# An SSM stage reordered: input tables ahead of output tables, an earlier forget gate, and stores issued by GpSimd

## The chip, the cores and the metric

One core of one Trainium2 chip runs the whole kernel. The metric is the device time of one execution in microseconds; a comparison goes by the median of several runs. Engines are named as the profile names them: PE is TensorE (matrix products), DVE is VectorE, ACT is ScalarE, POOL is GpSimd, SP is SyncE, which only issues transfers. ACT and POOL can issue transfers too; the profile writes an issue from ScalarE as ACTq, from SyncE as SPq.

## The reference

One block of a streaming encoder on 1024 rows and 16 meta rows (L = 1040) of width 1024: a root-mean-square norm, one large input projection, two mixers beside each other, gates, an output projection, and a gated feed-forward part with a short convolution. What matters here is the mixer:

```python
def _mixer(xn, w_in, b_forget, w_attn_out, lam_re, lam_im, b_re, ..., w_glu, w_o):
    proj = xn @ w_in
    q, k, v, f_logit, u, gates = jnp.split(proj, SPLITS, axis=-1)
    y_a = _forgetting_attention(q, k, v, f_logit, b_forget) @ w_attn_out
    z = jax.nn.gelu(_s5(u, lam_re, lam_im, b_re, b_im, c_re, c_im, d_skip, log_dt))
    zg = z @ w_glu
    y_s = zg[..., :D_MODEL] * jax.nn.sigmoid(zg[..., D_MODEL:])
    g = jax.nn.sigmoid(gates)
    merged = g[..., :D_MODEL] * y_a + g[..., D_MODEL:] * y_s
    return merged @ w_o
```

`_forgetting_attention` adds F[t] - F[s] to the logits, where F is the running sum of log sigmoid(f_logit + b_forget). `_s5` is a diagonal complex state space model (SSM): 32 groups of 16 channels with 64 complex states each, x_t = lam_bar x_(t-1) + b_bar u_t and y_t = Re(C x_t) + D u_t.

## The kernel before

Every matrix product of full precision is made of three products of rounded parts (xhi·whi, xlo·whi, xhi·wlo: `dense_steps`, lines 159 to 161, one "gate matmul" each below). The rounded weight whi is made by ScalarE from a loaded copy (raw, lines 140 and 146); its remainder wlo by a second load that GpSimd issues and that is added on top (`lo_by_dma`, lines 135 and 136). `split_lo` (line 129) is the same remainder made by VectorE or GpSimd. Since many places call it, its rows in the profile are told apart by the names of their tiles.

The stretch of interest lies between about 75 and 262 us.

- The **SSM input** u has been written to memory (u_d, line 394: steps 0 and 2 of it from SyncE, 1 and 3 from GpSimd).
- The **SSM** runs over the 32 groups in four steps qt = 0 to 3 of eight groups. In each, `tables` builds on VectorE two kinds of tables: the output tables Gm and Tm (16 matmuls of Gm with bA on line 1692 give Kt, copied by ScalarE on 1694; Tm is zeroed by GpSimd and filled by eight transfers of Kt from SyncE on 1702), and the input table (Vm, transposed by TensorE on 1713 and copied to Wi by ScalarE on 1714), and the decay dt8 (a copy on line 1716). `chain` loads U from u_d (1724), multiplies it with Wi (16 products, 1730, copied to wr and wi), runs the recurrence over the chunks on VectorE (two scans, and the complex rotations rot), and forms Y = Gm·St + Tm·U (1770 and 1772), its GELU, and the store y_d.
- The **gate chunks** are the dense work: eight chunks of 128 output channels, each three blocks of 342 columns with 24 matmuls: 576 in all. A sigmoid (443) and a store to g_d (444) follow every block. The SSM's products are mixed into this stream.
- Behind them stand **q and k** of the first pair of heads (`project_qk`, 144 matmuls), the **forget gate** (`forget`, lines 511 to 531: 48 products with wf, then Exp, Ln and a scan) and the **GLU** with w_glu, in the form of seven products of sums and differences of blocks of z and of the weights (`glu`, `seven`, lines 219 to 221; the weights' parts are the tiles ops, line 578).
- `load_z` (543 to 567) reads y_d back as zt in four pieces m, each by eight transfers, rounds them to zhi (548) with remainder zlo, forms the differences zf (558 to 561) and splits them in z1h, z1l, z2h and so on.

The order of instructions on each engine isn't the order of the text: a scheduler interleaves them at build time by priority and by its own estimate of what is ready, and `after` adds an order by hand. Every engine then executes its own list strictly in that order. A transfer's issue may wait for an older transfer, as there are a limited number of lanes by which their completion is told.

Of the kernel before, what the change touches and what calls it, by code (L numbers as in the profile page):

```python
# [19 lines left out]
P = 128  # L20
# [5 lines left out]
H = 8  # L26
# [24 lines left out]
def block_kernel(ctx, tc, x, meta, g1, x0t, g1t, w_q, w_k, w_v, w_f, w_u, w_g, b_f, w_ao, lam_d, bw_d, cw_d,  # L51
# [76 lines left out]
    def split_lo(eng, out_, src, hi):  # L128
        return eng.tensor_tensor(out_, src, hi.bitcast(F), ALU.subtract)  # L129
# [36 lines left out]
    def run(gen):  # L166
        for _ in gen:
            pass
# [234 lines left out]
        after(ld, queue[-1])  # L403
    next(ssm_steps)
    after(ssm_log[n_log], ready)
    ssm_tables, ssm_chain = next(ssm_steps)


    chains = {}

    def begin(q):
        ssm_tables(q)
        chains[q] = ssm_chain(q)
        next(chains[q])

    begin(0)
    begin(1)
    for q in range(4):
        run(chains[q])
        if q < 2:  # L420
            begin(q + 2)
    st_u.close()
    st_n.close()


    st_g = ExitStack()
    gp_ = pool(st_g, "gates", side="right")

# [2 lines left out]
    def gate_chunk(i, pl, tanh):  # L431
        whi, wlo = gate0[1:] if i == KD else wchunk(w_g[i], KD, GP, act=not tanh)
        if tanh:
            gs = pl.tile([P, LQ], F, tag="gs", name="gs", bufs=1)
        for t, n in QBLK:
            ps = mm_ps()
            yield from dense_steps(ps[:, :n], whi, wlo, xhi[:, :, T0 + t:T0 + t + n],
                                   xlo[:, :, T0 + t:T0 + t + n], KD)
            if tanh:
                S.activation(gs[:, t:t + n], ps[:, :n], AF.Tanh, scale=0.5)  # L440
            else:
                gs = pl.tile([P, LQ // 3], F, tag="gs", name="gs", bufs=2)
                S.activation(gs, ps[:, :n], AF.Sigmoid)
                S.dma_start(g_d[P * i:P * i + P, t:t + n], gs)
        if tanh:
            GP.tensor_scalar(gs, gs, 0.5, 0.5, ALU.mult, ALU.add)
            if pl is not gp_ and i == KD - 1:
                okeep["g"] = gs
            else:
                SY.dma_start(g_d[P * i:P * i + P], gs)  # L450
# [2 lines left out]
        run(gate_chunk(i, gp_, False))  # L453
    st_g.close()
    st_s.close()
    st_f = ExitStack()
    fp = pool(st_f, "fgate", side="right")
    fraw = fp.tile([P, KD, H], F, name="fraw")
    wf = fp.tile([P, KD, 64], R, name="wf")
    bf = fp.tile([H, 1], F, name="bf")  # L460

    def forget_w():
        SY.dma_start(fraw, w_f)
        SY.dma_start(bf, b_f.unsqueeze(1))
        GP.memset(wf.bitcast(F), 0.0)
        GP.tensor_scalar(wf[:, :, :H], fraw, 1.0, 0.0, ALU.mult, ALU.add)
        split_lo(GP, wf[:, :, 32:32 + H], fraw, wf[:, :, :H])

    st_k = ExitStack()
    qps = [pool(st_k, "qkA", side="left")]

# [34 lines left out]
    def zblock(r, h_):  # L508
        return [t_[:, 2 * r:2 * r + 2, TH * h_:TH * h_ + TH] for t_ in (zhi, zlo)]

    def forget():

        fl_ = gz.tile([P, L], F, tag="gl", name="fl_", bufs=2)[:H]
        fx = gz.tile([P, L], F, tag="gl", name="fx", bufs=2)[:H]
        for t, n in BLK:
            ps = mm_ps()
            for i in range(KD):
                PE.matmul(ps[:64, :n], wf[:, i, :], xhi[:, i, t:t + n], start=(i == 0), stop=False)
                PE.matmul(ps[:64, :n], wf[:, i, :], xlo[:, i, t:t + n], start=False, stop=(i == KD - 1))
            S.copy(fx[:, t:t + n], ps[32:32 + H, :n])  # L520
            V.scalar_tensor_tensor(out=fl_[:, t:t + n], in0=ps[:H, :n], scalar=bf, in1=fx[:, t:t + n],
                                   op0=ALU.add, op1=ALU.add)
        V.scalar_tensor_tensor(out=fx, in0=fl_, scalar=-1.0, in1=fl_, op0=ALU.mult, op1=ALU.max)
        S.activation(fx, fx, AF.Exp, scale=-1.0)
        S.activation(fx, fx, AF.Ln, bias=one[:H])
        V.scalar_tensor_tensor(out=fx, in0=fl_, scalar=0.0, in1=fx, op0=ALU.min, op1=ALU.subtract)
        V.tensor_tensor_scan(fl_, one[:H].broadcast_to([H, L]), fx, 0.0, ALU.mult, ALU.add)
        GP.tensor_scalar(fx, fl_, -8.0, 0.0, ALU.mult, ALU.add)
        SY.dma_start(f_d, fx)
        if "f_d" in dbg:  # L530
            SY.dma_start(dbg["f_d"], fx)

    def fold(t_):
        return t_.rearrange("p (n j) -> p j n", j=CH)

    def load_z():
        zts = []
        for m in range(4):
            tag = "gl" if m % 2 else "ms"
            zt = gz.tile([P, CH, NCH], F, tag=tag, name="zt", bufs=2)  # L540
            ym = y_d[m].rearrange("(j c) g n -> g c j n", c=GC)
            for g in range(GQ):
                SY.dma_start(zt[GC * g:GC * g + GC], ym[g])
            zts.append(zt)
        for m in range(4):
            w_ = NC2 if m < 2 else NCH
            zh, zl = (fold(t_[:, m, :CH * w_]) for t_ in (zhi, zlo))
            S.copy(zh, zts[m][:, :, :w_])
            split_lo(V, zl, zts[m][:, :, :w_], zh)

        def part(r, h_, k):
            return zts[2 * r + k][:, :, NC2 * h_:NC2 * h_ + NC2]

        T4 = zblock(0, 1)
        for k in range(2):
            fa, fb = (gz.tile([P, L], F, tag="cg", name="zf", bufs=2) for _ in range(2))
            f1, f2, f3, f4 = (fold(f_[:, TH * q:TH * q + TH]) for f_ in (fa, fb) for q in range(2))
            V.tensor_tensor(f1, part(0, 1, k), part(0, 0, k), ALU.subtract)
# [44 lines left out]

    n_used = [0]
    T4 = load_z()
    forget_w()
    qk = qk_tiles(0)
    run(project_qk(0, qk))
    forget()
    st_f.close()  # L610
    slots = []
    for q in range(4):
        t_ = wp.tile([P, 2, 2, 2, P], R, tag="wlo" if q % 2 else "whi", name="ops")
# [831 lines left out]
def ssm(tc, after, sp, s_ps, ident, u_d, y_d, lam_d, bw_d, cw_d, d_sk, l_dt):  # L1445
# [18 lines left out]
    def big(tag, shape, name=None):  # L1464
        return sp.tile(shape, F, tag=tag, name=name or tag, bufs=bufs[tag])
# [19 lines left out]
    def rest():  # L1485
# [183 lines left out]
        HQ = GQ // 2  # L1669
        state = {}  # L1670

        def tables(qt):
            g0 = qt * GQ
            Gm = big("Gm", [P, GQ, CH + 1, GC])
            tm = big("tq", [P, GQ, CH + 1, GC], "tm")

            def bcx(t_, n):
                return t_[:, g0:g0 + GQ].unsqueeze(2).broadcast_to([P, GQ, n, GC])
# [1 line left out]
            def bcp(t_, n):  # L1680
                return t_[:, :n, g0:g0 + GQ].rearrange("p t g -> p g t").unsqueeze(3).broadcast_to([P, GQ, n, GC])

            TT(Gm, bcx(cA, CH + 1), bcp(pr, CH + 1), ALU.mult)
            TT(tm, bcx(cB, CH + 1), bcp(pi, CH + 1), ALU.mult)
            TT(Gm, Gm, tm, ALU.subtract)
# [14 lines left out]
            GP.memset(Tm, 0.0)  # L1700
            for j in range(CH):
                SY.dma_start(Tm[16 * j:16 * (j + 1), :, 16 * j:], Kt[:, :, :P - 16 * j])

            Vm = big("tq", [P, GQ, CH, GC], "Vm")
            tv = big("tq", [P, GQ, CH, GC], "tv")
            TT(Vm, bcx(bA, CH), bcp(qr, CH), ALU.mult)
# [3 lines left out]
            for q in range(GQ // 4):  # L1710
# [1 line left out]
                for i in range(4):  # L1712
                    PE.transpose(wt[:, P * i:P * i + P], Vm[:, 4 * q + i].rearrange("p t c -> p (t c)"), ident)
                S.copy(Wi[:, 4 * q:4 * q + 4].rearrange("p g m -> p (g m)"), wt)
            dt8 = big("dt8", [P, HQ, NCH])
            V.tensor_copy(dt8, dec[:, qt * HQ:qt * HQ + HQ].unsqueeze(2).broadcast_to([P, HQ, NCH]))
            GP.memset(dt8[:, :, 0:1], 0.0)
            state[qt] = (Gm, Tm, Wi, dt8)

        def chain(qt):  # L1720
            g0 = qt * GQ
            Gm, Tm, Wi, dt8 = state.pop(qt)
            U = big("U", [P, GQ, NCH])
            SY.dma_start(U, u_d[qt])
            wr, wi = (big(n, [P, HQ, NCH]) for n in ("wr", "wi"))
            for e in range(2):
                for q in range(0, HQ, 2):
# [5 lines left out]
                    S.copy(wr[64 * e:64 * e + 64, q:q + 2], w3[:64])  # L1733
                    S.copy(wi[64 * e:64 * e + 64, q:q + 2], w3[64:])
            yield
            rc, rs = (t_[:, qt % 2 * HQ:qt % 2 * HQ + HQ] for t_ in rot[qt // 2])
            ta, tb = (big(n, [P, HQ, NCH]) for n in ("ta", "tb"))
            TT(ta, wr, rc, ALU.mult)
# [14 lines left out]
            for part, (op, fa, fb) in enumerate(((ALU.subtract, wr, ta), (ALU.add, ta, wr))):  # L1753
# [3 lines left out]
                for e in range(2):  # L1757
                    r_ = slice(64 * e, 64 * e + 64)
                    TT(S4[64 * part:64 * part + 64, :, e, 1:], x_[r_, :, :NCH - 1], y_[r_, :, :NCH - 1], op)
            if qt == 0:  # L1760
                n_ = len(log)
                rot.append(rotation(1))
                after(log[n_], log[n_ - 1])
            Y = big("sy", [P, GQ, NCH], "Y")
            for q in range(0, GQ, 3):
                nq = min(3, GQ - q)
# [5 lines left out]
                    PE.matmul(yo, Tm[:, q + i, :], U[:, q + i, :], start=False, stop=True)  # L1772
                S.copy(Y[:, q:q + nq].rearrange("p a n -> p (a n)"), yps[:, :NCH * nq])
            S.activation(Y, Y, AF.Gelu_apprx_tanh)
            S.dma_start(y_d[qt], Y)

        yield tables, chain

    return log, loads, rest()

# [56 lines left out]
```

## Time and profile before

| | us |
|---|---|
| runs before | 1481.59, 1489.31, 1491.31 (median 1489.31) |
| profiled execution, first to last instruction (span) | 1485.7 |
| TensorE busy | 1440.4 (97%), 9712 matmuls |
| VectorE busy | 1071.4 (72%) |
| ScalarE busy | 712.2 (48%) |
| GpSimd busy | 742.1 (50%) |

The profiled execution's own device time isn't listed beside its span; the median of the runs is 3.6 us above that span. "Busy" counts the time in which an instruction of the engine runs; matmuls overlap, so the time of one (0.32 us) is longer than its step (about 0.16 us). PEclk is the clock that TensorE was granted, as a share of full speed. In the lists of waits a row says who waited, for which instruction, for how long in all, how often and how long at most.

### The profile page before, as it was taken

Reading aid. Unit: us, or ns where it says so; the run is one execution under the profiler, and the core shown is the slowest. Engines: PE = TensorE matmul, PEld = TensorE weight load, DVE = VectorE, ACT = ScalarE, POOL = GpSimd, SP = SyncE. Lnnn points to the kernel's source line nnn. Section 1 sums busy time; section 2 is a strip of 40 time slices with the busy share of each in tenths; the row PEclk is TensorE's granted clock in tenths of the full one; section 3 lists DMA queues with packets and bytes.
Section 4 is the critical chain, followed back from the end, with each engine's and each line's share of the span. In section 5 each row is a group of like instructions: output and inputs, shape, how many; then the busy total and the mean of one; then the engine's idle time right before and its main releaser. Section 6 shows DMA issues by size and latency. Waiting matters only on the chain. (4 is left out here: it accounts for less than half of the span.)

```text
span 1485.7 us, 26584 instructions
## 1 busy us (share of the span) xinstructions
PE 1440.4 (97%) x9712; PEld 1358.8 (91%) x9712; DVE 1071.4 (72%) x2173; ACT 712.2 (48%) x1384; POOL 742.1 (50%) x850
## 2 busy tenths in 40 slices
PE   7999997999999999999999999999999999998997
PEld 7989996998899999999888999999999999777886
DVE  6879648881566676647468987888877776788785
ACT  6434675541555665543546534444444445543433
POOL 1311125752456465524863144455544426789766
PEclk9999999999999999999999999999999999999999
DMA  6366571551127342047885135676653215765513
GB/s 246 86 157 157 128 163 50 177 160 43 48 79 178 93 111 90 26 148 256 257 158 185 57 109 141 178 199 188 174 143 100 84 57 180 286 203 148 168 40 114
DMA packets 91032, 206.72 MB, mean 139 GB/s; under 512 B 14651, under 2 KB 25531, under 8 KB 90517
## 3 DMA queue, kind: packets, MB, share of 16 engines
q1 hardware_dynamic: 69380, 159.73, 32.9%
q0 software_dynamic: 15296, 34.63, 13.2%
q10 hardware_dynamic: 6224, 10.65, 1.9%
q8 instruction: 77, 1.26, 0.3%
q14 instruction: 55, 0.44, 0.1%
HBM read 165.90 MB, written 69.35 MB: 158 GB/s over the span
## 5 line engine op out<-in xcount | busy, mean ns | idle before, releaser
L159 PE MATMUL mm<-xhi,whi 128*128 128x342 f32 (+2 forms) x488 | 159.4, 327 | 1.0 <-DVE q L129 1.0
L161 PE MATMUL mm<-xhi,wlo 128*128 128x342 f32 (+2 forms) x488 | 158.3, 325 | 0.0
L160 PE MATMUL mm<-xlo,whi 128*128 128x342 f32 (+2 forms) x488 | 157.7, 324 | 0.0
L1079 POOL TENSOR_TENSOR ov<-ov,og 128x1024 f32<-128x1024 f32 x21 | 51.1, 2434 | 125.6 <-ACT og L1078 121.7
L129 DVE TENSOR_TENSOR sw<-sf,sw 128x512 fp32r<-128x512 f32 x72 | 66.6, 925 | 50.0 <-ACT sw L1070 49.8
L1070 ACT CAST sw<-sf 128x512 fp32r<-128x512 f32 x72 | 44.9, 624 | 106.2 <-POOL sf L1196 74.5
L159 PEld LDWEIGHTS mm<-xhi,whi 128*128 128x128 f32 x488 | 91.9, 188 | 2.1 <-PE sp L714 0.8
L161 PEld LDWEIGHTS mm<-xhi,wlo 128*128 128x128 f32 x488 | 91.8, 188 | 0.3
L160 PEld LDWEIGHTS mm<-xlo,whi 128*128 128x128 f32 x488 | 91.9, 188 | 0.2
L763 ACT CAST th<-tp 128x256 fp32r<-128x256 f32 (+3 forms) x120 | 56.2, 472 | 62.5 <-PE tp L756 30.1
L129 DVE TENSOR_TENSOR tl<-tp,th 128x256 fp32r<-128x256 f32 (+3 forms) x120 | 65.2, 547 | 25.1 <-ACT th L763 23.7
L1196 POOL TENSOR_TENSOR sf<-raw,sf 128x512 f32<-128x512 f32 x36 | 59.1, 1641 | 44.8 <-DVE sw L129 44.7
L1196 POOL TENSOR_TENSOR sf<-raw 128x512 f32<-128x512 f32 x36 | 48.0, 1332 | 66.9 <-DMA raw<-in_w_up_dram 35.9
L221 PE MATMUL mm<-xhi,sw 128*128 128x258 f32 (+1 forms) x288 | 81.0, 281 | 0.0
L219 PE MATMUL mm<-xhi,sw 128*128 128x258 f32 (+1 forms) x288 | 80.8, 281 | 0.0
L220 PE MATMUL mm<-xlo,sw 128*128 128x258 f32 (+1 forms) x288 | 80.7, 280 | 0.0
L728 POOL TENSOR_SCALAR pt<-pt,nm 128x144 f32<-128x144 f32 (+4 forms) x72 | 51.8, 731 | 48.5 <-DVE nm L727 47.5
L1248 DVE SCALAR_TENSOR_TENSOR ov<-hv,cwt,ov 128x1024 f32<-128x1024 f32 x36 | 72.5, 2014 | 0.1
L1070 ACT CAST sw<-raw 128x512 fp32r<-128x512 f32 x70 | 43.0, 621 | 53.3 <-PE sp L221 25.5
L726 ACT ACTIVATE pt<-pt,nm 128x144 f32<-128x144 f32 (+4 forms) x72 | 52.9, 735 | 26.1 <-DVE nm L725 25.7
L719 DVE CUSTOM_DVE_ANT_0 pt<-sp,fb 128x328 f32<-128x328 f32 (+8 forms) x112 | 46.4, 430 | 20.0 <-PE sp L714 11.1
L756 PE MATMUL tp<-ident,pt 128*128 128x128 f32 (+1 forms) x360 | 58.3, 270 | 0.1
(708 smaller groups left out, 5702.1 us busy)
## 6 DMA issues: line engine op xcount, KB each, us to landing
raw<-in_w_up_dram SPq DMA_DIRECT2D x44, 512.0 KB, 3.6
t_d<-in_w_dn_dram POOLq DMA_DIRECT2D x44, 256.0 KB, 7.0
ar<-a_d SPq DMA_DIRECT2D x44, 256.0 KB, 5.1
wr<-t_d SPq DMA_DIRECT2D x44, 256.0 KB, 2.8
a_d<-ov SPq DMA_DIRECT2D x21, 512.0 KB, 2.6
wr<-in_w_dn_dram SPq DMA_DIRECT2D x33, 256.0 KB, 3.8
t_d<-in_w_dn_dram SPq DMA_DIRECT2D x22, 256.0 KB, 4.2
t_d<-t_d SPq DMA_DIRECT2D x22, 256.0 KB, 4.7
```

The costliest lines, as they stand in the source:

```text
L129: return eng.tensor_tensor(out_, src, hi.bitcast(F), ALU.subtract)
L159: yield PE.matmul(ps, whi[:, i, :], ahi[:, i], start=(i == 0), stop=False)
L160: yield PE.matmul(ps, whi[:, i, :], alo[:, i], start=False, stop=False)
L161: yield PE.matmul(ps, wlo[:, i, :], ahi[:, i], start=False, stop=(i == k - 1))
L219: PE.matmul(ps, a[0][:, i], bh, start=(i == 0 and not joins), stop=False, skip_group_check=True)
L220: PE.matmul(ps, a[0][:, i], bl, start=False, stop=False, skip_group_check=True)
L221: PE.matmul(ps, a[1][:, i], bh, start=False, stop=(i == kh - 1), skip_group_check=True)
L756: PE.transpose(tp[:kn, o:o + n], p_[:n, k0:k0 + kn], ident[:n, :n])
L763: S.copy(th[:kn, z:tw], tp[:kn, z:tw])
L1070: S.copy(hi, src)
L1196: sums.append(GP.tensor_tensor(f_, a, b, op))
L1248: V.scalar_tensor_tensor(out=o, in0=h_[:, j:SEQ + j], scalar=cwc(j, m), in1=o, op0=ALU.mult, op1=ALU.add)
```

## The change

Four things, and none of them alters the arithmetic:

1. `tables` is cut into `input_tables` (Vm, Wi) and `output_tables` (Gm, Kt, Tm). A step begins with its input table and the load of U; its output tables come behind the U·Wi products (before the scans of that step), except for step 0, whose output tables follow at once. The second half of the rotation moves from the end of step 0 to the start of step 2.
2. The decay's copy is made by ScalarE in `chain`, behind the U·Wi products.
3. The forget gate's weights are loaded and converted by GpSimd ahead of the gate chunks, and its 48 products and what follows come right behind the gate chunks, ahead of q and k. It has tiles of its own.
4. The stores of g_d, y_d and f_d, the loads of the forget gate's weights, and every second of the eight loads of z's last piece are issued by GpSimd.

```diff
     begin(0)
+    ssm_out(0)
     begin(1)
     for q in range(4):
+        next(chains[q])
+        if q:
+            ssm_out(q)
         run(chains[q])
         if q < 2:
             begin(q + 2)
...
+    fraw = fp.tile([P, KD, H], F, name="fraw")
+    wf = fp.tile([P, KD, 64], R, name="wf")
+    bf = fp.tile([H, 1], F, name="bf")
+    GP.memset(wf.bitcast(F), 0.0)
+    for ld in (GP.dma_start(fraw, w_f), GP.dma_start(bf, b_f.unsqueeze(1))):
+        after(ld, late[0])
+    GP.tensor_scalar(wf[:, :, :H], fraw, 1.0, 0.0, ALU.mult, ALU.add)
+    split_lo(GP, wf[:, :, 32:32 + H], fraw, wf[:, :, :H])
...
                 S.activation(gs, ps[:, :n], AF.Sigmoid)
-                S.dma_start(g_d[P * i:P * i + P, t:t + n], gs)
+                GP.dma_start(g_d[P * i:P * i + P, t:t + n], gs)
...
     for i in range(KD, 2 * KD):
         run(gate_chunk(i, gp_, False))
     st_g.close()
     st_s.close()
...
+    fw = pool(st_f, "fwork", side="right")
+    fl_, fx = (fw.tile([H, L], F, name=nm) for nm in ("fl_", "fx"))
+    forget()
+    st_f.close()
...
             for g in range(GQ):
-                SY.dma_start(zt[GC * g:GC * g + GC], ym[g])
+                (GP if m == 3 and g % 2 else SY).dma_start(zt[GC * g:GC * g + GC], ym[g])
...
     T4 = load_z()
-    forget_w()
     qk = qk_tiles(0)
     run(project_qk(0, qk))
-    forget()
-    st_f.close()
...
-            dt8 = big("dt8", [P, HQ, NCH])
-            V.tensor_copy(dt8, dec[:, qt * HQ:qt * HQ + HQ].unsqueeze(2).broadcast_to([P, HQ, NCH]))
-            GP.memset(dt8[:, :, 0:1], 0.0)
-            state[qt] = (Gm, Tm, Wi, dt8)
+            state[qt] = [Wi]
...
             yield
+            dt8 = big("dt8", [P, HQ, NCH])
+            S.copy(dt8, dec[:, qt * HQ:qt * HQ + HQ].unsqueeze(2).broadcast_to([P, HQ, NCH]))
+            GP.memset(dt8[:, :, 0:1], 0.0)
+            if qt == 2:
+                rot.append(rotation(1))
             rc, rs = (t_[:, qt % 2 * HQ:qt % 2 * HQ + HQ] for t_ in rot[qt // 2])
...
-            if qt == 0:
-                n_ = len(log)
-                rot.append(rotation(1))
-                after(log[n_], log[n_ - 1])
+            yield
+            _, Gm, Tm = state.pop(qt)
             Y = big("sy", [P, GQ, NCH], "Y")
...
             S.activation(Y, Y, AF.Gelu_apprx_tanh)
-            S.dma_start(y_d[qt], Y)
+            GP.dma_start(y_d[qt], Y)
```

As the scheduler lays it out, the number of instructions stays the same in all (ScalarE's 28 store issues move to GpSimd, four copies from VectorE to ScalarE, and seven issues from SyncE to GpSimd). On TensorE the first U·Wi products come behind 44 gate matmuls instead of 85, the products for Kt of step 0 behind 58 instead of 23, and Y of step 0 behind 210 instead of 209. Behind the last gate matmul come 48 products of the forget gate, then 144 of q and k, then the GLU; before it was q and k, forget gate, GLU. From about 262 us on, all engines have the same order as before.

More of the change, by code (lines that the diff above doesn't have):

```diff
@@ L405, in block_kernel @@
     after(ssm_log[n_log], ready)
-    ssm_tables, ssm_chain = next(ssm_steps)
+    ssm_in, ssm_out, ssm_chain = next(ssm_steps)
     chains = {}
     def begin(q):
-        ssm_tables(q)
+        ssm_in(q)
         chains[q] = ssm_chain(q)
@@ L423, in block_kernel @@
     st_n.close()
+    st_f = ExitStack()
+    fp = pool(st_f, "fgate", side="right")
+    fraw = fp.tile([P, KD, H], F, name="fraw")
[6 more added lines that the diff above has]
+    split_lo(GP, wf[:, :, 32:32 + H], fraw, wf[:, :, :H])
     st_g = ExitStack()
@@ L455, in block_kernel, with forget @@
     st_s.close()
[L456 to L467, printed above, removed]
+    def forget():
+        for t, n in BLK:
+            ps = mm_ps()
+            for i in range(KD):
+                PE.matmul(ps[:64, :n], wf[:, i, :], xhi[:, i, t:t + n], start=(i == 0), stop=False)
+                PE.matmul(ps[:64, :n], wf[:, i, :], xlo[:, i, t:t + n], start=False, stop=(i == KD - 1))
+            S.copy(fx[:, t:t + n], ps[32:32 + H, :n])
+            V.scalar_tensor_tensor(out=fl_[:, t:t + n], in0=ps[:H, :n], scalar=bf, in1=fx[:, t:t + n],
+                                   op0=ALU.add, op1=ALU.add)
+        V.scalar_tensor_tensor(out=fx, in0=fl_, scalar=-1.0, in1=fl_, op0=ALU.mult, op1=ALU.max)
+        S.activation(fx, fx, AF.Exp, scale=-1.0)
+        S.activation(fx, fx, AF.Ln, bias=one[:H])
+        V.scalar_tensor_tensor(out=fx, in0=fl_, scalar=0.0, in1=fx, op0=ALU.min, op1=ALU.subtract)
+        V.tensor_tensor_scan(fl_, one[:H].broadcast_to([H, L]), fx, 0.0, ALU.mult, ALU.add)
+        GP.tensor_scalar(fx, fl_, -8.0, 0.0, ALU.mult, ALU.add)
+        GP.dma_start(f_d, fx)
+        if "f_d" in dbg:
+            SY.dma_start(dbg["f_d"], fx)
+    fw = pool(st_f, "fwork", side="right")
+    fl_, fx = (fw.tile([H, L], F, name=nm) for nm in ("fl_", "fx"))
+    forget()
+    st_f.close()
     st_k = ExitStack()
@@ L509, in zblock @@
         return [t_[:, 2 * r:2 * r + 2, TH * h_:TH * h_ + TH] for t_ in (zhi, zlo)]
[L511 to L531, printed above, removed]
     def fold(t_):
@@ L1670, in rest, with views @@
         state = {}
-        def tables(qt):
+        def views(qt):
             g0 = qt * GQ
-            Gm = big("Gm", [P, GQ, CH + 1, GC])
-            tm = big("tq", [P, GQ, CH + 1, GC], "tm")
             def bcx(t_, n):
@@ L1681, in bcp, with output_tables @@
                 return t_[:, :n, g0:g0 + GQ].rearrange("p t g -> p g t").unsqueeze(3).broadcast_to([P, GQ, n, GC])
+            return g0, bcx, bcp
+        def output_tables(qt):
+            g0, bcx, bcp = views(qt)
+            Gm = big("Gm", [P, GQ, CH + 1, GC])
+            tm = big("tq", [P, GQ, CH + 1, GC], "tm")
             TT(Gm, bcx(cA, CH + 1), bcp(pr, CH + 1), ALU.mult)
@@ L1702, in tables, with input_tables @@
                 SY.dma_start(Tm[16 * j:16 * (j + 1), :, 16 * j:], Kt[:, :, :P - 16 * j])
+            state[qt] += Gm, Tm
+        def input_tables(qt):
+            g0, bcx, bcp = views(qt)
             Vm = big("tq", [P, GQ, CH, GC], "Vm")
@@ L1714, in tables @@
                 S.copy(Wi[:, 4 * q:4 * q + 4].rearrange("p g m -> p (g m)"), wt)
-            dt8 = big("dt8", [P, HQ, NCH])
-            V.tensor_copy(dt8, dec[:, qt * HQ:qt * HQ + HQ].unsqueeze(2).broadcast_to([P, HQ, NCH]))
-            GP.memset(dt8[:, :, 0:1], 0.0)
-            state[qt] = (Gm, Tm, Wi, dt8)
+            state[qt] = [Wi]
         def chain(qt):
-            g0 = qt * GQ
-            Gm, Tm, Wi, dt8 = state.pop(qt)
+            Wi, = state[qt]
             U = big("U", [P, GQ, NCH])
@@ L1774, in chain @@
             S.activation(Y, Y, AF.Gelu_apprx_tanh)
-            S.dma_start(y_d[qt], Y)
-        yield tables, chain
+            GP.dma_start(y_d[qt], Y)
+        yield input_tables, output_tables, chain
     return log, loads, rest()
```

## The prediction

> **What bounds the kernel now.** I read the head of the page first, then the table of busy time by stage for the stretch that the change touches, then the waits of TensorE in it, then the timelines around each wait.
>
> ```profile
> span 1485.7 us, 26584 instructions
> PE 1440.4 (97%) x9712; PEld 1358.8 (91%) x9712; DVE 1071.4 (72%) x2173; ACT 712.2 (48%) x1384; POOL 742.1 (50%) x850
> ```
>
> TensorE has work in 1440.4 of 1485.7 us. The change neither adds nor removes a matmul, so it can only move TensorE's idle time (45.3 us in all) and the stretches in which its clock is halved. After about 262 us every engine has the same instructions in the same order in both kernels; what TensorE is late by there it stays late by. So I follow TensorE from 75 to 262 us.
>
> ```profile
> core 0: us, PE busy (x) PEld busy (x) DVE busy (x) ACT busy (x) POOL busy (x), PEclk, DMA share, GB/s
> 80.10:89.90 9.80, 9.80 (x66) 9.71 (x65) 6.84 (x20) 1.88 (x3) 1.58 (x3) 1.00 1.07 214
> 93.70:97.10 3.40, 3.40 (x16) 3.40 (x16) 2.69 (x6) 1.64 (x5) 0.15 (x2) 0.50 0.33 90
> 122.00:202.00 80.00, 80.00 (x566) 78.78 (x566) 54.36 (x90) 46.86 (x74) 10.15 (x15) 1.00 0.60 152
> 201.60:224.60 23.00, 23.00 (x146) 22.84 (x144) 15.43 (x20) 17.95 (x28) 7.68 (x4) 1.00 0.68 133
> 227.60:233.60 6.00, 5.97 (x24) 5.24 (x25) 5.92 (x6) 2.73 (x6) 3.57 (x2) 0.50 0.01 3
> 233.60:237.90 4.30, 4.30 (x26) 3.34 (x25) 4.29 (x4) 3.17 (x9) 2.56 (x3) 0.99 0.42 118
> 238.00:245.30 7.30, 6.23 (x50) 5.82 (x49) 6.51 (x13) 3.68 (x8) 1.91 (x3) 1.00 0.00 1
> 247.60:254.00 6.40, 3.30 (x24) 2.87 (x24) 5.33 (x7) 2.68 (x7) 4.83 (x3) 1.00 0.00 0
> ```
>
> ```profile
> PE mm L518 <- POOL wf L129: 2.9, 1, 2.9
> PE sp L1730 <- ACT Wi L1714: 2.7, 1, 2.7
> PE mm L221 <- DVE ops L129: 1.7, 1, 1.7
> PE mm L219 <- ACT ms L232: 1.2, 1, 1.2
> PE tp L219 <- DVE cg L225: 1.2, 1, 1.2
> PE mm L219 <- DVE kl L129: 0.9, 1, 0.9
> ```
>
> Six waits make almost all of the idle time here: 2.7 us before the first U·Wi product of the SSM, 2.9 us before the forget gate, and 5.0 us (1.7, 1.2, 1.2, 0.9) in the first GLU products. The first two leave the clock at 0.50 behind them, for 3.4 us (1.7 us lost) and about 6.0 us (3.0 lost). That is about 15 us, 1.0% of the span, and bounds any gain from above: 1% is also about what a measurement of this kernel can tell from no change.
>
> **Part 1: input tables ahead of output tables.** The first U·Wi needs two things, Wi (the input table) and U (read back from memory).
>
> ```profile
> 77.34 1.05 PE L1692 MATMUL sp<-Gm,sm 128*16 128x128 f32 x8
> 79.19 0.58 PE L160 MATMUL mm<-xlo,g 128*128 128x342 f32 x2
> ...
> 88.20 0.32 PE L161 MATMUL po<-xhi,wlo 128*128 128x342 f32 x1
> ...
> 89.80 0.32 PE L159 MATMUL po<-xhi,whi 128*128 128x342 f32 x1
> 92.83 0.71 PE L1730 MATMUL sp<-U,Wi 128*128 128x130 f32 x4 [2.72 <-ACT Wi L1714]
> ```
>
> ```profile
> 79.14 1.18 SPq L1724 DMA_DIRECT2D U<-u_d  x2
> U<-u_d SPq DMA_DIRECT2D x4, 520.0 KB, 13.2
> 90.62 1.53 ACTq L444 DMA_DIRECT2D g_d<-gs  x2
> 92.19 0.59 ACT L1714 COPY Wi<-sp 128x512 f32<-128x512 f32 x1 [8.10 <-DMA U<-u_d]
> ```
>
> The wait is put down to the copy of Wi, but ScalarE reached that copy late because its two g_d stores were held until a load of U had landed. U was issued at 79.14 and the load takes about 13 us (DMA share 1.07 in the 80.1 to 89.9 row), so it is in place at about 79.1 + 12.6 = 91.7; the 12.6 is the shortest of the four loads, whose median is the 13.2 shown, and I take it because the first of the pair leads. In the changed order U·Wi comes after 44 gate matmuls instead of 85, and ahead of the 16 small products of the output table. The rows at 88.20 and 89.80 are ten steps of gate matmuls apart, 0.160 us each; 41 of them are 6.6 us, and the small products take 79.19 - 77.34 = 1.85 us. TensorE would therefore ask for U at 90.1 - 6.6 - 1.85 = 81.7. The issue of U does not move: ahead of it on SyncE stand the same sixteen u_d stores. So TensorE waits 91.7 - 81.7 = 10.0 us where it waited 2.7: **+7.3 us**. All that was cover (the 41 matmuls, the table's products) is done later instead of under the load. ScalarE no longer holds its stores behind this load, which gives at most the 1.1 us from 91.7 to 92.8, already in the 91.7. The traffic that leaves the window (eight Tm transfers and two stores) is small beside two U loads of 520 KB, so U may land up to 3 us earlier, no more: range +4.3 to +7.3.
>
> Clock behind it: the wait of 2.7 us was followed by 3.4 us at half, that of 2.9 by 6.0. After 10 us I put the loss between the same 1.7 and 3.0, that is **+0.8** (0 to 1.3).
>
> Later in the gate stage I walked the four steps. U·Wi of steps 2 and 3 now has about 5.9 us from the issue of U to its use, and the Tm of steps 1 and 3 about 11 us from the table's products to Y.
>
> ```profile
> 139.97 7.79 SPq L1702 DMA_DIRECT2D Tm<-Kt  x8
> ...
> 167.91 6.47 SPq L1702 DMA_DIRECT2D Tm<-Kt  x8
> Tm<-Kt SPq DMA_DIRECT2D x4, 16.0 KB, 3.6
> ```
>
> Issuing the eight pieces takes 6.5 to 7.8 us and the last ones land some 3.6 us later, so 10 to 11.4 us plus the copies of Kt: each Tm is on time or 1 to 2 us late. A load of U at 13.2 (the median) would be late by 7, but the traffic is light by then (share 0.60 in the row from 122 to 202). Together 0 to +7, **I take +2**, near the low end, since each of four waits is small. The decay's copy moves 0.43 us a step from VectorE to ScalarE, half idle in this stage; it hides there and would cost that 0.43 four times if it did not.
>
> **Part 2: forget gate behind the gate chunks.** Its weights are now loaded and converted far ahead, so the 2.9 us wait on wf goes, and with it the half clock behind (6.0 us at 0.50): **-5.9 us**. That is firm unless something else makes TensorE wait at the end of the gate stage. The forget gate's scan, Exp and Ln leave the GLU stage and fall into q's projection, where VectorE had a hole:
>
> ```profile
> 205.71 0.89 DVE L129 TENSOR_TENSOR q<-mm,q 64x272 fp32r<-64x272 f32 x2 [15.13 <-ACT q L487]
> ```
>
> They are hidden there. But q and k now run behind the forget gate, and in the changed order ScalarE copies z (into zhi) behind the copies of q's last block. Before, those copies lay between the blocks of q.
>
> ```profile
> L548 ACT CAST zhi<-zt 128x1040 fp32r<-128x1040 f32 x2 | 4.7, 2345 | 0.0
> L548 ACT CAST zhi<-zt 128x520 fp32r<-128x520 f32 x2 | 2.5, 1236 | 2.3 <-DMA zt<-y_d 2.3
> L129 DVE TENSOR_TENSOR zlo<-zt,zhi 128x1040 fp32r<-128x1040 f32 x2 | 4.6, 2304 | 0.0
> L558 DVE TENSOR_TENSOR zf<-zt 128x520 f32<-128x520 f32 x2 | 2.7, 1363 | 0.1
> L129 DVE TENSOR_TENSOR z1l<-zf,z1h 128x520 fp32r<-128x520 f32 x2 | 1.9, 944 | 0.0
> L129 DVE TENSOR_TENSOR ops<-sf,ops 128x256 fp32r<-128x256 f32 x8 | 3.8, 479 | 1.2 <-ACT ops L578 1.1
> ```
>
> Counted from the end of the gate stage (201.6 before): the forget gate takes 3.0 + 4.3 = 7.3 us at full clock (its two rows), q and k 23.0, half of it q. So q's last block ends at about 7.3 + 11.5 = 18.8, TensorE reaches the GLU at 30.3. ScalarE needs 1.7 for q and two weight copies, then 1.2 + 1.2 + 2.3 + 2.3 = 7.1 for zhi: done at 27.6. VectorE closes its last zlo at 29.9, then has four splits of the differences (0.8 each by their 0.7 to 0.9; the row of z1l is the highest), two weight splits, the first zf of the next half and one weight split more (3.2 + 1.0 + 1.4 + 0.5 = 6.1): 36.0. The eleventh GLU product needs that last weight, and TensorE would be there at 30.3 + 1.2 = 31.5: a wait of about 4.5 us. The next weight on ScalarE stands behind k's twelve copies and costs about 2.5 more, and two small ones 1.0: 8.0 in all. Against the 5.0 us of GLU waits before, of which the later ones stood behind the scan, Exp and Ln that are now gone: 8.0 + 1 (what may be left of those) - 5.0 = **+4**. The bounds are -5.0 (z is always ahead, all waits gone) and +9.
>
> The row from 247.6 to 254.0 shows TensorE idle for 3.1 of 6.4 us in pieces, with the clock still at 1.00, so I add no half clock here. The Trainium skill, "TensorE: Matmul & The Clock Gate", Part 1 (What's actually happening), says that the clock falls to half after an idle window of about 3.4 us, and that the windows run freely; by it a wait of 4.5 us can cost up to 1.7 more, and the sum would be 10 instead of 8. The trace is harsher than the rule on one point: waits of 2.7 and 2.9 us already left 0.50 behind them.
>
> **Part 3: stores on GpSimd.** The 24 g_d and four y_d stores leave ScalarE's queue, and four of z's loads SyncE's.
>
> ```profile
> g_d<-gs ACTq DMA_DIRECT2D x24, 171.0 KB, 3.3
> wlo<-in_w_g_dram POOLq DMA_DIRECT2D x7, 512.0 KB, 7.3
> 204.33 0.87 POOL L136 DMA_DIRECT2D wlo<-in_w_k_dram  x1 [10.99 <-ACT wlo L135]
> ```
>
> GpSimd's issue of a large load takes 0.87 us, and it then waits 11 us for the next, so 28 issues of under 0.9 us fit into the 120 us of the gate stage (10.15 us busy in 80). ScalarE gets nothing back that TensorE waited for, except the block in part 1. What is queued behind: each wlo load of the next weights now stands behind the store of a gate block, which waits for its sigmoid and for an older transfer to land. Lateness of one or two us is within the margins I found (1 to 3 us): **0**, bounds -1 and +8 (the third rival).
>
> **Sum.** 7.3 + 0.8 + 2 - 5.9 + 4 + 0 = +8.2 us on a span of 1485.7. The profiled execution's device time is not listed beside its span; the three runs have a median of 1489.3, 3.6 above the span, and I add the 8.2 to that: 1497.5.
>
> **The rivals.**
> - *GLU never waits, U lands early.* The point from which it decides: with U 3 us earlier the GLU waits of the new order must stay under 5.8 us, with U as forecast under 2.8. They do if zhi is not held behind q, that is if the copies of z run as soon as their loads land; z's first three pieces are in memory before the gate stage ends. Against it stands the fixed order on ScalarE. Price: U 3 us earlier (4.3), clock 0.8, the wf wait -5.9, GLU -4 (1 us of waits left), no late tables: -4.8, so 1484.5: not slower. Chance 0.20.
> - *The change pays in full.* U's wait does not grow because the load itself starts or lands 7 us earlier. Nothing in the trace lets it start earlier; then 15 us would be gained at most: 1474. Chance 0.05.
> - *GpSimd's queue is late.* Behind a store that waits, a weight load that lands in 7.3 us is issued 2 to 3 us later, and a gate chunk starts late in four of the seven: +8 to +10, so 1506. For it speaks VectorE's load in this stage (54.36 of 80 us); against it that GpSimd was idle in most of it. Chance 0.20. The Trainium skill, "DMA: Bandwidth & Descriptors", SWDGE vs HWDGE vs iDMA, speaks for it: descriptors of GpSimd's transfers are written to memory that VectorE locks in its two-port mode, while those of ScalarE and SyncE are not. No row of before shows such a lock.
> - *Tables and U of later steps late as well.* The upper ends of part 1 (+7) and of the GLU (+9): 7.3 + 1.3 + 7 - 5.9 + 9 = 18.7, so 1508. Chance 0.10.
>
> **How the numbers follow.** The forecast has 0.45. Its own range is 1491 to 1504. A part of it (0.06) and nearly all of the third and fourth (0.25 of 0.30) lie above 1504.2, so slower by over 1% gets 0.31; faster by over 1% only the second, 0.05; the rest, 0.64, is within 1%. The range for 8 in 10 goes from just under the first rival, 1484, to a little above the fourth, 1512.
>
> **What would show it.** Right: in the profile after, a wait of TensorE on U of 9 to 10 us near 82 us, with the clock at 0.5 behind; no wait on wf; waits at the first GLU products on the weights that VectorE splits; the GLU reached 2 to 6 us later than at 238. Wrong: U's wait under 6 us (part 1), no GLU wait (part 2), or waits at the gate chunks for wlo (part 3).

## The result and the profile after

The changed kernel is slower: a median of 1500.45 us over four runs (1498.73 to 1503.36) against 1487.01 us for the kernel before in the same comparison, a ratio of 1.0084 with a 95% interval of 1.0061 to 1.0108. That is +13.4 us where +8.2 was forecast, inside the range and within 1%. One execution of the kernel before and one of forget_only, further down, ran slow (1761 and 1765 us at a granted clock of 0.75) and are left out of every median and ratio here.

The head of the page after, then TensorE's waits between 75 and 262 us (who waited, for what, total, times, longest):

```profile
span 1499.6 us, 26593 instructions
PE 1447.2 (97%) x9712; PEld 1365.5 (91%) x9712; DVE 1070.4 (71%) x2169; ACT 713.8 (48%) x1388; POOL 757.7 (51%) x885
```

```profile
PE sp L1731 <- DMA U<-u_d: 8.5, 1, 8.5
PE tp L1776 <- DMA raw<-in_w_glu_dram: 4.1, 1, 4.1
PE sp L221 <- DVE ops L129: 2.5, 1, 2.5
PE tp L219 <- ACT ops L579: 2.4, 1, 2.4
PE sp L220 <- DVE z2l L129: 1.8, 1, 1.8
PE mm L219 <- DVE kl L129: 0.2, 1, 0.2
```

The wait on wf is gone, and so is the old one on Wi. In their place stand 8.5 us on U, 4.1 us before Y of step 3 (line 1776 is Tm·U), and 6.9 us in the first GLU products. The table by stage shows what came behind each wait:

```profile
core 0: us, PE busy (x) PEld busy (x) DVE busy (x) ACT busy (x) POOL busy (x), PEclk, DMA share, GB/s
72.50:81.00 8.50, 8.50 (x53) 8.26 (x52) 8.18 (x28) 1.66 (x3) 4.86 (x8) 0.93 0.98 232
81.00:89.50 8.50, 0.06 (x1) 0.00 (x0) 6.42 (x11) 0.00 (x0) 2.63 (x5) 0.67 1.06 254
89.50:94.20 4.70, 4.66 (x20) 4.69 (x21) 0.00 (x0) 3.01 (x9) 0.00 (x0) 0.51 0.11 40
94.20:200.00 105.80, 105.80 (x735) 102.99 (x734) 77.39 (x131) 55.06 (x94) 24.65 (x45) 1.00 0.51 124
200.00:204.10 4.10, 0.02 (x2) 0.04 (x1) 0.00 (x0) 0.00 (x0) 0.00 (x0) 0.91 1.05 269
204.10:210.30 6.20, 6.20 (x28) 6.20 (x29) 0.00 (x0) 1.17 (x3) 0.00 (x0) 0.51 1.17 142
215.00:245.50 30.50, 30.50 (x194) 29.28 (x192) 19.89 (x21) 21.46 (x30) 9.40 (x12) 1.00 0.41 76
245.50:260.00 14.50, 7.59 (x35) 6.61 (x35) 14.27 (x21) 10.18 (x24) 8.76 (x6) 0.69 0.25 85
```

Two waits, and behind each a stretch at clock 0.51: 4.7 us of work behind U (2.3 lost) and 6.2 us behind the late Tm (3.1 lost). The gate stage begins at 72.5 (73.5 before) and ends at 215.0 (201.6 before), so from its first matmul it lasts 142.5 us instead of 128.1: +14.4. The idle time and the clock account for it: 8.5 - 2.7 on U, 4.1 on Tm, 2.3 - 1.7 and 3.1 at half clock, and 0.6 in the 72.5 to 81.0 row (0.07 of 8.5) make 14.2. The forget gate, q and k then take 30.5 us instead of 36.3 (-5.8); from the first GLU product to the 400th it is 59.6 us instead of 55.0 (+4.6). Sum +13.1, from a start 1.0 earlier, so +12.1 by the 400th GLU product. The span grew by 13.9: 1.8 came later still, and a fall of the clock near 1383 us (0.83 in the row from 1378 to 1388), which the profiled run of the kernel before doesn't have, makes 1.7 of it (more on this under forget_only).

Why Tm is late can be read from the way of Kt, SyncE's issues and the landings of the last pieces:

```profile
187.03 1.05 PE L1694 MATMUL tp<-Gm,sm 128*16 128x128 f32 x8
...
189.80 0.56 ACT L1696 COPY Kt<-tp 16x512 f32<-16x512 f32 x1
...
191.65 7.53 SPq L1704 DMA_DIRECT2D Tm<-Kt  x8
...
Tm<-Kt SPq DMA_DIRECT2D x1, 24.0 KB, 6.0
Tm<-Kt SPq DMA_DIRECT2D x1, 8.0 KB, 6.5
```

From the first product for Kt to the first issue it is 4.6 us: ScalarE reaches the copies of Kt right behind the GELU of step 2, at 189.8. The eight pieces take 7.5 us to issue, the last begins at 197.2 and takes 6.5 to land, at 203.7: TensorE waits until 204.1. The row of waits names a load of GLU weights; it shares a completion counter with the pieces of Tm.

### The profile page after: what moved, and what is told of

It is laid out like the page before. It is cut to its first block, busy times and chain, and to the rows that moved or that the text cites. A ratio compares the mean times of both kernels' runs of the same rounds, so it can differ in the third digit from the quotient of the medians.

```text
span 1499.6 us, 26593 instructions
## 1 busy us (share of the span) xinstructions
PE 1447.2 (97%) x9712; PEld 1365.5 (91%) x9712; DVE 1070.4 (71%) x2169; ACT 713.8 (48%) x1388; POOL 757.7 (51%) x885
## 3 DMA queue, kind: packets, MB, share of 16 engines
q0 software_dynamic: 17632, 41.29, 14.2%
## 5 line engine op out<-in xcount | busy, mean ns | idle before, releaser
L160 PEld LDWEIGHTS mm<-xlo,whi 128*128 128x128 f32 x480 | 90.6, 189 | 0.2
L717 DVE CUSTOM_DVE_ANT_0 pt<-sp,fb 128x328 f32<-128x328 f32 (+8 forms) x112 | 46.4, 430 | 20.2 <-PE sp L712 12.1
L129 DVE TENSOR_TENSOR sw<-raw,sw 128x512 fp32r<-128x512 f32 x70 | 54.5, 781 | 5.9 <-ACT sw L1068 5.2
```

Source lines behind the costliest of these rows:

```text
L160: yield PE.matmul(ps, whi[:, i, :], alo[:, i], start=False, stop=False)
```

## The experiments

All ratios are against runs of the kernel before on the same chip. The two columns in the middle come from the timelines of the profiled runs: the length of the gate stage (first gate matmul to the first matmul behind the gates) and of the stage behind it (to the 400th GLU product).

| kernel | gate stage | stage behind | median us | ratio [95%] |
|---|---|---|---|---|
| before | 128.1 | 91.4 | 1487.0 to 1488.7 | 1 |
| changed | 142.5 | 90.1 | 1500.45 | 1.0084 [1.0061, 1.0108] |
| ssm_only | 137.5 | 96.9 | 1502.69 | 1.0110 [1.0094, 1.0126] |
| forget_only | 126.5 | 89.5 | 1487.84 | 1.0000 [0.9986, 1.0014] |
| stores_only | 127.2 | 91.0 | 1486.63 | 0.9987 [0.9975, 0.9999] |
| late_uwi | 133.2 | 90.2 | 1490.76 | 1.0020 [1.0009, 1.0031] |
| tm_two_queues | 136.5 | 89.8 | 1497.70 | 1.0069 [1.0051, 1.0087] |
| z_ahead | 142.2 | 91.4 | 1501.49 | 1.0093 [1.0075, 1.0112] |
| three_orders | 128.9 | 91.4 | 1488.50 | 1.0013 [0.9999, 1.0027] |
| wf_early | 126.2 | 91.9 | 1488.97 | 1.0009 [0.9994, 1.0024] |
| gp_after | 129.8 | 93.4 | 1492.15 | 1.0027 [1.0016, 1.0038] |
| gp_forget | 125.3 | 92.3 | 1488.24 | 1.0000 [0.9988, 1.0011] |
| u1_behind_tm | 141.4 | 90.1 | 1498.87 | 1.0066 [1.0049, 1.0083] |

**One part at a time.** Each of the first three kernels is the kernel before with one part of the diff: the split of the tables with the decay's copy; the forget gate with its early weights; the lines with GP for g_d, y_d and zt.

ssm_only: 

> Only the first two parts of the change (input tables ahead, decay's copy on ScalarE); forget gate and stores as before. Theory: the 13 us come from lost cover: U waited for 8.5 us near 82 us (5.8 more than before) with about 0.6 more at half clock, and the Tm of step 3 late, here 71 gate matmuls behind its small products instead of 65, so 3 us of wait and about 3 us at half clock; the forget gate's wait on wf (2.9) stays and the GLU waits stay at about 5. Sum +12 us against before (between +8 and +15). Rival (the stores on GpSimd carry the loss): +4 us or less here.

forget_only: 

> Only the forget gate and its weights moved; SSM order and stores as before. Theory: the wf wait and its half clock go (-5.9 us), and the copies of z fall behind q's last block, so the GLU waits and half clock give +4.4 back: -1.5 us against before (between -4 and +1), with TensorE waits of 6 to 8 us in the first GLU products. Rival (the GLU waits come from z's last piece being late through GpSimd's queue, not from the order on ScalarE): no growth of the GLU waits here, -6 us.

stores_only: 

> Only the stores of g_d and y_d and four of z's loads moved to GpSimd. Theory: nothing but the copy of Wi, which is no longer held behind stores, so the wait of 2.7 us near 90 us falls to about 1.6: -1 us against before (between -2 and +1). Rival (GpSimd's queue is late): +4 us or more, with TensorE waiting at gate matmuls for wlo.

Measured by the medians: +14.2, -0.6 and -1.9 us, which sum to +11.7 beside the 13.4 of the whole (by the ratios +16.4, 0 and -1.9, so +14.5 beside 12.5: the sum agrees within the noise, no closer). The loss lies in the SSM's part. The rival that the stores carry it is out. In ssm_only TensorE waited 9.1 us on U; its Tm was only 1.6 us late, and the rest came as waits in the stage behind (96.9 us), which the theory had not placed there: one for wlo of k (1.8), the others in the GLU. The wait on wf, expected to stay, is not among them. So the size came near the forecast, the place of a third of it did not:

```profile
PE sp L1737 <- DMA U<-u_d: 9.1, 1, 9.1
PE sp L220 <- DVE z2l L129: 2.9, 2, 2.3
PE mm L219 <- DVE kl L129: 2.4, 1, 2.4
PE tp L219 <- DVE cg L225: 2.1, 1, 2.1
PE po L161 <- DMA wlo<-in_w_k_dram: 1.8, 1, 1.8
PE tp L1782 <- DMA g_d<-gs: 1.6, 1, 1.6
```

forget_only has the GLU waits of the changed kernel with z's loads all on SyncE, so these waits come from the order and not from GpSimd's queue. By the 400th GLU product its profiled run is ahead of the one before by 3.4 us, and at the end by 0.6 only: near 1367 us the clock falls (0.83 in the 1360 to 1380 row against 1.00 before), with the same busy time. That is no property of this kernel alone: the row from 1360 to 1390 has the clock between 0.89 and 0.94 in every profiled run but those of before and ssm_only, where it is 1.00. So a profile set beside that one profile of the kernel before looks 1.7 to 3.4 us worse by it (3.4 or 6.8 us at half clock); whether the unprofiled runs of before have the stretch isn't on record.

```profile
1360.00:1380.00 20.00, 16.98 (x63) 13.40 (x62) 19.31 (x25) 9.45 (x18) 14.16 (x10) 0.83 1.02 283
```

**U·Wi of step 0 behind cover.** The changed kernel with step 1's input table built first and an order on TensorE:

```diff
-    begin(0)
-    ssm_out(0)
-    begin(1)
+    ssm_in(0)
+    ssm_out(0)
+    ssm_in(1)
+    for q in range(2):
+        chains[q] = ssm_chain(q)
+        next(chains[q])
...
+            after(first_u_wi_of_step_0, last_transpose_of_Vm_of_step_1)
```

> The changed kernel with one more order: the U.Wi products of step 0 behind the input table of step 1, so behind 76 gate matmuls instead of 43. Theory (lost cover): TensorE asks for U 5 to 7 us later, the wait on U falls from 8.5 to about 2 us, the rest as in the changed kernel: 6 us faster than the changed kernel, +7 us against before. Rival (U lands late for another reason, and the wait only moves to the U of step 1, whose products follow at once): less than 3 us faster than the changed kernel.

By the two ratios it is 9.5 us faster than the changed kernel, more than forecast. TensorE's idle row before U·Wi of step 0:

```profile
90.56 0.68 PE L1735 MATMUL sp<-U,Wi 128*128 128x130 f32 x4 [1.57 <-DMA U<-u_d]
```

The wait fell from 8.5 to 1.6 us with U landing no earlier (90.6 against 89.5 us), and no half clock followed it. The Tm of step 3 was also less late (2.7 instead of 4.1 us, with 3.4 instead of 6.8 us at half clock behind). So the lost cover is shown, and the rival that the wait moves to the next step is out. (With this order the Tm of step 0 is also issued earlier, at 81.8 instead of 98.8 us; TensorE waited for it in neither run.)

**Tm from two queues.** The changed kernel with

```diff
-                SY.dma_start(Tm[16 * j:16 * (j + 1), :, 16 * j:], Kt[:, :, :P - 16 * j])
+                (S if j % 2 else SY).dma_start(Tm[16 * j:16 * (j + 1), :, 16 * j:], Kt[:, :, :P - 16 * j])
```

> The changed kernel with the eight Tm transfers of each step issued from two queues, SyncE and ScalarE by turns. Theory (the issue of eight pieces, 5.5 to 7.5 us from one queue, makes Tm late): the wait of 4.1 us before Y of step 3 falls under 1.5 and the 6.8 us at half clock behind it go: -5 to -6 us against the changed kernel, about +8 against before. Rival (the landing of the last pieces, up to 6.5 us beside z's loads and the weights, makes it late): less than 2 us gained.

```profile
PE sp L1731 <- DMA U<-u_d: 9.5, 2, 8.8
PE mm L219 <- DVE kl L129: 3.3, 1, 3.3
PE mm L219 <- ACT c L228: 1.9, 1, 1.9
```

The wait on Tm is gone altogether and the gate stage is 6.0 us shorter, as forecast; that the eight pieces left from one queue is what made Tm late. The last piece now begins 2.6 us behind the first instead of 5.6, and lands in 3.9 us instead of 6.5; the run doesn't tell the two apart. The median fell by less (the ratio from 1.0084 to 1.0069, intervals that overlap), so the gain on the whole time is not measured well.

**z's copies ahead of q's.** The changed kernel with an order on ScalarE (`after` on the four copies of z): q's second block behind the third copy, q's third block and the first eight copies of GLU weights behind the fourth.

> The changed kernel with one more order on ScalarE: the four copies of z (zhi) before the second and third block of q, and the first GLU weights behind them. Theory (the GLU waits because z's copies stand behind q's last block): zhi starts some 5 us earlier, the GLU waits of 6.9 us fall to 2 or 3 and the 10.2 us at half clock shrink: -5 us against the changed kernel (-3 to -8). Rival (VectorE's and ScalarE's work of this stretch is as long as TensorE's, so the wait only moves on to k's splits or to the weights): less than 2 us gained.

```profile
248.50 0.66 PE L159 MATMUL mm<-xhi,whi 128*128 128x384 f32 x1 [6.49 <-DVE q L129]
```

The rival held. The GLU waits fell to 1.8 us, but k's last block now waited 6.5 us for a bank that q had not left. The stage behind the gates was no shorter (91.4).

**The three orders together.** The first two orders as above; of the third, q's second block stays where it was, and only its third block and the GLU weights go behind z's copies.

> The changed kernel with all three: U.Wi of step 0 behind the input table of step 1, Tm from two queues, z's copies ahead of q's later blocks. Theory: the gains add where they touch different waits: -10 (measured for the first alone), -4 (the wait of 2.7 us on Tm that was left there and 1.7 at half clock), -5: 1482 us, that is -5 against before. Rival (the waits move on): -10 to -12 against the changed kernel, no better than before.

```profile
PE sp L219 <- ACT ops L588: 4.7, 1, 4.7
```

10.6 us by the ratios and 12 by the medians faster than the changed kernel, and level with the one before (the interval reaches from 0.9999 to 1.0027): the rival's number. The gate stage is back at 128.9, and the stage behind at 91.4, with 4.7 us of wait for a GLU weight of ScalarE and 1.8 for k's split where the gain of 5 was expected.

**The early weights alone.** The kernel before with the forget gate's load and conversion moved ahead of the gates, and nothing else.

> The kernel before with the forget gate's weights loaded and converted ahead of the gate chunks, as in the change, and nothing moved. Theory (after q and k the stretch is bound by VectorE's splits of z, k and the GLU weights): the wait on wf of 2.9 us and its half clock go, and come back in part as waits on the splits of k: -2 us against before (-4 to 0). Rival (the term of -5.9 us as the prediction has it): -5 to -6.

```profile
PE mm L513 <- DVE kl L129: 4.1, 1, 4.1
PE sp L1724 <- ACT Wi L1708: 2.4, 1, 2.4
PE mm L221 <- DVE ops L129: 1.7, 1, 1.7
PE mm L219 <- DVE kl L129: 1.5, 1, 1.5
```

No gain. The wait of 2.9 us on wf became 4.1 and 1.5 us on k's splits, and the stage still lasts 91.9 us; the -2 of the forecast is not there. Behind the wait on wf, another one had been hidden that ended no earlier: the GLU begins 36.4 us behind the gates, and 36.3 in the kernel before.

**Work taken from VectorE.** Two of z's four remainders zlo made by GpSimd: in gp_after on the changed kernel with the late U·Wi and two queues, in gp_forget on the kernel before with the other two parts of the change.

```diff
-            split_lo(V, zl, zts[m][:, :, :w_], zh)
+            split_lo(GP if m > 1 else V, zl, zts[m][:, :, :w_], zh)
```

> The changed kernel with U.Wi of step 0 behind the input table of step 1, Tm from two queues, and two of the four remainders zlo of z made by GpSimd instead of VectorE. Theory (after the gates VectorE sets the pace, so work taken from it comes off the end): VectorE loses 4.6 us of work there, GLU waits of about 7 us fall to 3, the half clock shrinks: 1484 us, -4 against before, where the same without GpSimd would be near 1488. Rival (ScalarE's copies, in the same order, set the pace): 1487 to 1489.

> The kernel before with the stores on GpSimd, the forget gate moved as in the change, and two of the four zlo made by GpSimd. Theory (VectorE's pace): the forget gate alone measured 0 and the stores -2; with 4.6 us less on VectorE the GLU waits fall by 3 to 4: 1483 us, -5 against before. Rival (ScalarE's copies set the pace, or GpSimd is slow at it): 1486 to 1488.

gp_forget came to 1488.2, the rival's number, gp_after to 1492.2, worse than both. GpSimd's own row and three of VectorE's in gp_after, then GpSimd's in gp_forget:

```profile
229.22 14.42 POOL L129 TENSOR_TENSOR zlo<-zt,zhi 128x1040 fp32r<-128x1040 f32 x2
...
231.53 0.68 DVE L129 TENSOR_TENSOR z1l<-zf,z1h 128x520 fp32r<-128x520 f32 x1
...
238.06 2.82 DVE L565 TENSOR_TENSOR zf<-zt,zf 128x520 f32<-128x520 f32 x1
...
242.06 2.13 DVE L129 TENSOR_TENSOR z1l<-zf,z1h 128x520 fp32r<-128x520 f32 x1
```

```profile
224.04 6.89 POOL L129 TENSOR_TENSOR zlo<-zt,zhi 128x1040 fp32r<-128x1040 f32 x2 [2.09 <-ACT zhi L545]
```

A zlo that takes VectorE 2.3 us took GpSimd 3.4 and 3.7 us in gp_forget, but 10.7 and 3.8 in gp_after. Some of VectorE's own work on z ran longer beside it (2.8 and 2.1 us for operations that took 1.7 and 0.8 in the changed kernel), some did not (0.68 at 231.5, beside the same zlo). So these runs did not take a clean 4.6 us from VectorE, and do not tell whether VectorE or ScalarE sets the pace. Why one zlo took 10.7 us stays open, and the changed kernel with only the late U·Wi and the two queues, from which the theory counts, was not run.

**How long U takes to land.** Two tries. The first ordered the load of step 1 behind the U·Wi products of step 0:

> The changed kernel with the load of U of step 1 issued behind the U.Wi products of step 0, so that the load of step 0 runs without it. Theory A (the two loads of 520 KB run piece by piece beside each other, so that each takes the time of both): U of step 0 lands 4 to 6 us earlier, the wait of 8.5 us falls to 3 to 5. Theory B (the load shares the engines with all that is in flight, two weight chunks and the u_d stores above all): 1 to 2 us earlier. In both the half clock behind the wait (10.2 us) may shrink by one step of 3.4, and a late U of step 1 could cost up to 2.

Its order on SyncE stayed as it was (both loads were issued within 2.4 us), so its 1.0085 tells nothing. The second ordered it behind the Tm of step 0, on the same engine:

> The changed kernel with the load of U of step 1 issued behind the Tm transfers of step 0 (near 105 us), so that the load of step 0 is alone on SyncE's queue; the U.Wi of step 1 stands behind 147 gate matmuls instead of 128. Theory A (the two loads run piece by piece beside each other): U of step 0 lands 4 to 6 us earlier, the wait of 8.5 us falls to 3 to 5 and the half clock behind it shrinks: -5 us against the changed kernel or more. Theory B (the load shares the engines with everything in flight, u_d stores and weights above all, of which the second load is 0.5 of some 3 MB): 1 to 2 us earlier, -2 us. In both a late U of step 1 could cost up to 2.

```profile
78.48 0.46 SPq L1725 DMA_DIRECT2D U<-u_d  x1
91.11 1.21 PE L1733 MATMUL sp<-U,Wi 128*128 128x130 f32 x4 [8.49 <-DMA U<-u_d]
```

U of step 0 alone still needs 12.6 us, and the wait is 8.5 as before. Theory A is out, and not even B's 1 to 2 us are seen; the time fell by some 2 us (the intervals overlap), about what the less late Tm (2.8 us) gives. The DMA share was 1.04 between 82 and 90 us here, with the eight u_d stores of GpSimd (landing in 11.3 us) and the weight loads in flight. In the changed kernel the loads of steps 2 and 3 took 3.1 and 4.2 us.

There is a rival that neither theory has and no run tests: SyncE's own u_d stores, issued just ahead of U. The lists of transfers issued from 74 to 94 us, changed kernel and u1_behind_tm:

```profile
u_d<-usb SPq DMA_DIRECT2D x4, 65.0 KB, 13.2
```

```profile
u_d<-usb SPq DMA_DIRECT2D x7, 65.0 KB, 12.5
```

These stores of 65 KB take as long as the 520 KB of U behind them. The last of them landed at 88.8 us in the changed kernel, where TensorE started on U at 89.5, and at 90.3 in u1_behind_tm, where it started at 91.1; in the kernel before it landed at 90.7 and U at 91.7. So most of the 13 us may be the wait behind these stores, eight of which belong to step 2, whose U is loaded only at 128 us. Issuing those behind the load of step 0 would test it.

## Why the prediction was right, point by point

- **U's wait: right.** Forecast 10.0 us, +7.3; measured 8.5, +5.8. TensorE asked at 81.0 (81.7 forecast). U was issued at 76.5 and not at 79.1, so "the issue does not move" was off by 2.6 us, 1.0 of which the whole stretch ran earlier; the 13 us of the load held. Two readings behind it did not: the 12.6 is not the shortest of four loads, since the trace tells only two landings, both of the pair near 79 us (12.6 and 13.7); and so the 13.2 says nothing of the later steps, whose loads took 3.1 and 4.2 us in the changed kernel. What the 13 us consist of was not in the prediction, and stays open.
- **Clock behind it: right.** +0.8 forecast, +0.6 by the 89.5 to 94.2 row.
- **Late tables: the failed step.** I took +2 of 0 to 7, "each Tm is on time or 1 to 2 us late". Three of the four waits named there did not occur, but Tm of step 3 cost 4.1 us and 3.1 at half clock: 7.2. Three things were missing. The sum of 10 to 11.4 us "plus the copies of Kt" gave these copies no size: from the first product for Kt to the first issue it is 4.6 us after, and was 5.7 in the same step before (162.16 to 167.91). The last piece took 6.5 us to land, where I used 3.6; that was the median of one size over all four steps, and before, too, the last piece of step 3 took 6.4:

```profile
162.16 1.05 PE L1692 MATMUL sp<-Gm,sm 128*16 128x128 f32 x8
...
Tm<-Kt SPq DMA_DIRECT2D x1, 8.0 KB, 6.4
```

  And a wait of 4 us also left half clock behind it. So the rows of before already made the way of Kt and Tm 17.5 us in step 3, against the 11 that I had found between the products and Y (13.0 after, to the moment when TensorE asked). This term is 5.2 us too small, as much as the whole miss; that the others nearly cancel (-1.5 on U, -0.2 on the clock behind it, +0.6 on the GLU, +0.6 of half clock at the start of the stage that nobody forecast) is luck.
- **Forget gate: right in its place, and misleading.** Forget gate, q and k lasted 5.8 us less (5.9 forecast), the GLU 4.6 more (4 forecast). ScalarE's copies of z began at 235.8, that is 20.8 us after the gates (20.5 forecast), and the eleventh product's weight came 36.5 us after them (36.0):

```profile
235.76 6.67 ACT L549 CAST zhi<-zt 128x520 fp32r<-128x520 f32 x4
...
251.47 0.80 PE L221 MATMUL sp<-z2h,ops 128*128 128x260 f32 x2 [2.53 <-DVE ops L129]
```

  The size of the GLU term is partly luck: I had counted 9 us of waits and no half clock, and there were 6.9 us of waits and 10.2 us at half clock, with 7.3 us of work in them (3.6 lost). And the two terms are not independent, as I had them. In eleven of the twelve kernels of the table beside the one before, whatever wait was taken out, the stage lasts between 89.5 and 93.4 us. So the rival of a GLU that never waits would hardly have gained its 5 us either: in z_ahead, where the GLU waits fell to 1.8 us, a wait turned up at k.
- **Stores: right.** 0 forecast with bounds from -1 to +8; -1.9 measured. TensorE's waits of stores_only name no gate weight. The Trainium skill, "DMA: Bandwidth & Descriptors", SWDGE vs HWDGE vs iDMA, which spoke for the rival of a late GpSimd queue, is not contradicted, but no run here shows such a cost: g_d landed in 3.8 us from GpSimd against 3.3 from ScalarE.
- **The clock gate.** I added no half clock for the GLU waits, by the row from 247.6 to 254.0 of before, and it cost 3.6 us: the 245.5 to 260.0 row has the clock at 0.69. The Trainium skill, "TensorE: Matmul & The Clock Gate", Part 1 (What's actually happening), has the clock fall to half after an idle window of about 3.4 us; the 1.7 us that I had estimated from this rule were nearer than the nothing that I used, though no single wait here was as long as such a window (2.5 us at most).

What sets the 90 us of the stage behind the gates stays open. VectorE is busy in 36.2 of 41.6 us there and ScalarE in 29.8 (changed kernel, 220.4 to 262), but neither was relieved cleanly.

No version beat both kernels by more than 0.13%: stores_only, the one part of the change that may help a little, is at 0.9987 [0.9975, 0.9999].

## What to carry to other kernels

Before moving a product ahead, ask for the arrival of each of its operands, not of the one that the profile names: the wait was put down to Wi, and U arrived only 1.1 us before TensorE started. Work that is moved ahead of a transfer's arrival takes the cover away from that transfer, at the price of that cover less what the transfer itself comes earlier (here 2.3 us). And a wait that is taken out is worth only its distance to the next one: take it out by itself in a run before counting its length as gain.

## What the runs showed of the hardware

- Waits of TensorE that are short or come in pieces can halve its clock too: 4.1 us of wait were followed by 6.2 us of work at 0.51, and 6.9 us in four pieces brought the 245.5 to 260.0 row down to 0.69. In the kernel before, 3.1 us in pieces within 6.4 us left it at 1.00.
- A subtraction of 128x1040 with a rounded result took GpSimd 3.4 to 3.8 us in three cases and 10.7 in one, where VectorE needs 2.3; some of VectorE's own operations ran nearly three times as long beside it (2.1 against 0.8 us), others as long as ever (0.68).
- A load of 520 KB took 12.6 to 13.0 us at a DMA share of 1.04 to 1.06 behind stores of the same queue that took 12.5 to 13.2 themselves, whether or not a second load of its kind followed; at other times it took 3.1 to 4.2 us.
